# A two-layer diffusion step on one core: the first shift row summed on VectorE, the later conditioning rows turned to columns one tile later

## The chip, the cores and the metric

The kernel runs on one core of a Trainium2 chip. The metric is the device time of one execution in microseconds; the time given for a kernel is the median of several runs. One further execution is recorded by the hardware profiler, and every row quoted here is from such a recording. A core has five engines that work through lists of their own: TensorE (PE, with its weight loads as PEld), VectorE (DVE), ScalarE (ACT), GpSimd (POOL) and SyncE (SP, which here issues the loads). They wait for each other by semaphores only.

## The reference

One inference step of a model with two layers on 1024 latent and 128 context tokens of width 1024. Layer 0 mixes with a bidirectional gated linear recurrence, layer 1 with attention; each is followed by a squared-ReLU MLP. What matters here is how the conditioning enters: each layer makes six rows of 1024 from a condition vector, two of them (shift and scale) ahead of each norm and one (gate) behind each branch.

```python
def adaln_params(cond, w_ada, b_ada):
    mod = jax.nn.silu(cond) @ w_ada + b_ada
    return jnp.split(mod, 6, axis=-1)

def modulate(h, shift, scale):
    return h * (1 + scale[:, None, :]) + shift[:, None, :]

for l in range(DEPTH):
    sh1, sc1, g1, sh2, sc2, g2 = adaln_params(cond, ada_w[l], ada_b[l])
    h = modulate(rms_norm(x, norm_mix[l]), sh1, sc1)
    x = x + g1[:, None, :] * mixer(h)
    h = modulate(rms_norm(x, norm_mlp[l]), sh2, sc2)
    x = x + g2[:, None, :] * sq_relu_mlp(h, mlp_w1[l], mlp_w2[l])
```

There are two condition vectors, one for the latent and one for the context tokens. In the text "row j" is row j of layer 0: 0 shift and 1 scale ahead of the recurrence, 2 its gate, 3 and 4 shift and scale ahead of the MLP, 5 its gate.

## The kernel before, in words

Activations lie transposed: 128 partitions by 8 blocks of the width, and the 1152 tokens in three chunks of 384. A dense product runs three float32r matmuls for each 128x128 block (L120, L123, L124): weights and activations are split into a high and a low part (`whi`/`wlo`, `hhi`/`hlo`). Weights come as 512 KB pieces (`raw`, L88), are split on ScalarE (L93) and on VectorE or GpSimd (L95), and are prefetched in the order in which they are used.

The code is traced in program order; the framework's scheduler then writes each engine's list and hands out the buffers of each tag, and an instruction that needs a buffer waits until one is released. Two tags matter. `bank` (L126) hands out the eight PSUM banks. `unit` (L487) hands out twelve buffers of 128x1152 in the first layer's recurrent half; there nearly all that is not an activation chunk takes one: the squares and their sums, the conditioning weights, the gates' tensors and the copied rows.

**Two ways to make a conditioning row.** On TensorE: `ada_mm` (L162) multiplies both condition vectors, held as columns `cs`, with a tile of 128 inputs by 1024 outputs (`ada_n`); eight such tiles sum up in two banks with two rows of 512 each. `ada_rows` (L169) then copies each bank to SBUF (ScalarE, L175), turns it into columns with four transposes (TensorE, L178) and adds the bias (`mod_finish`, VectorE, L199 and L202). On VectorE: `ada_dot` (L142) takes a tile of 128 outputs by 1024 inputs (`ada_wt`) and multiplies it with the condition vector, broadcast over the partitions as `cb`, with a running sum; there is one such instruction for each of the two conditions, and the result is a column at once.

**Start** (`first_half`, L401). The first chunk of `x` is loaded, squared and summed; then for k from 0 to 7 the weights of row 1 and row 0 are loaded (L429) and multiplied on TensorE. Within that loop the chunk's `rstd` (L220, matmuls at L226) is worked out at k = 2 and spread over the partitions (L254) at k = 4. `ada_rows` for row 1 and for row 0 follows, then `modulate` (L266) writes `hhi` (ScalarE, L278) and `hlo`, and the first dense groups begin.

**Recurrent stage** (`rglru`, L490). There are eight tiles n of 128 state channels. In each, TensorE runs a dense group x (n + 1), two chunk groups y, and the gates of tile n (`gates`, L522). After the gates' matmuls stand ScalarE's exponentials (L545), tanh (L550) and roots (L559), and VectorE's products and scans (L567). At the end of the tile `ada_pe(3)` (L181) takes the next three of the 24 weight tiles of rows 2, 3 and 4, through two buffers `adaw` (L184). So row 2 is complete in tile 2 (its eighth weight tile is the second of the three), row 3 in tile 5 (first of the three) and row 4 in tile 7. When a row is complete, `ada_rows` runs at once. The last groups y 6 and 7 of each chunk and the split of the products into `zhi` and `zlo` close the stage.

All other rows, row 5 of layer 0 and the six of layer 1, are made on VectorE during the output projection and the MLP (`ada`, L149), with `cb` loaded and passed through Silu in `rg_out` (L647, L648).

Of the kernel before, what the change touches and what calls it, by code (L numbers as in the profile page):

```python
# [7 lines left out]
F32 = mybir.dt.float32  # L8
F32R = mybir.dt.float32r
I32 = mybir.dt.int32  # L10
AF = mybir.ActivationFunctionType
# [4 lines left out]
D = 1024  # L16
# [36 lines left out]
ADA_PE = [(_j, _k) for _j in (2, 3, 4) for _k in range(8)]  # L53


class Emit:
# [85 lines left out]
    def ada_dot(self, w, l, j, k, *conds):  # L142
        for cond in conds:
            self.nc.vector.scalar_tensor_tensor(  # L144
                out=w if cond else self.junk, in0=w, scalar=1.0, in1=self.cb[:, cond],
                op0=ALU.mult, op1=ALU.mult, accum_out=self.mod[:, l, j, cond, k:k + 1],
            )

# [17 lines left out]
                ps[i][0:2], lhsT=self.cs[:, :, k], rhs=w[:, i * 512:(i + 1) * 512], start=(k == 0), stop=(k == 7)  # L166
            )

    def ada_rows(self, l, j, ps):  # L169

        nc = self.nc
        psm = self.bank(16)
        for i in range(2):
            srow = self.unit("srow")[0:2, :512]
            nc.scalar.copy(out=srow, in_=ps[i][0:2])  # L175
            for k in range(4):
                o = 2 * (4 * i + k)
                nc.tensor.transpose(psm[:, o:o + 2], srow[:, k * 128:(k + 1) * 128], self.ident[0:2, 0:2])  # L178
        self.mod_finish(l, j, psm)

    def ada_pe(self, n):  # L181
        for j, k in self.pe_jobs[:n]:
            w = self.rgt.tile([128, 1024], F32, tag="adaw", name="adaw", bufs=2)
            self.nc.sync.dma_start(w, self.I["ada_n"][j, k * 128:(k + 1) * 128])  # L184
            if k == 0:
                self.ada_ps = [self.bank(512) for _ in range(2)]
            self.ada_mm(self.ada_ps, w, k)
            if k == 7:
                self.ada_rows(0, j, self.ada_ps)
        del self.pe_jobs[:n]  # L190

    def mod_finish(self, l, j, ps=None):
# [208 lines left out]
    def first_half(self, stop):  # L401
        nc, tc, I = self.nc, self.tc, self.I
        self.rgt = self.alloc(name="rgt", bufs=1, side="right")
        self.cells = None
        self.pe_jobs = list(ADA_PE)
        self.cs = self.rgt.tile([128, 2, 8], F32, name="cs")
        nc.scalar.activation(out=self.cs, in_=self.v("cond", 0, 16), func=AF.Silu)
        xs, sts = [], [{} for _ in range(NCH)]
        H = []

        def load_x0(c):
            x = self.cbig(F32, "x0")
            nc.sync.dma_start(x, I["xt"][c])
            xs.append(x)

        def square(c, ks=range(KT)):
            for k in ks:
                self.sq_acc(sts[c], xs[c][:, k], k)

        def hpair():  # L420
            H.append((self.cbig(F32R, "hhi"), self.cbig(F32R, "hlo")))

        load_x0(0)
        square(0)
        ps = [[self.bank(512) for _ in range(2)] for _ in range(2)]
        for k in range(8):
            for j in (1, 0):
                w = self.unit("ada")[:, :1024]
                nc.sync.dma_start(w, I["ada_n"][j, k * 128:(k + 1) * 128])  # L429
                self.ada_mm(ps[j], w, k)  # L430
            if k == 2:
                y = self.rstd(sts[0], D)
            if k == 4:
                r = self.spread(y)
        self.prefetch(2)
        load_x0(1)
        load_x0(2)
        self.ada_rows(0, 1, ps[1])
        self.ada_rows(0, 0, ps[0])
        hpair()  # L440
        for k in range(KT):
            self.modulate(0, xs[0], r, 0, 0, *H[0], ks=[k])
            if k >= 4:
                square(1, [k - 4])
        self.prefetch(3)
        square(1, range(4, 8))
        square(2)
        hpair()
        hpair()
        gens = [None] + [self.norm_mod(c, xs[c], sts[c], 0, 0, *H[c]) for c in (1, 2)]  # L450
        for g in gens[1:]:
            next(g)
        self.rglru(H, gens)
        self.rg_out(H, stop)
# [35 lines left out]
    def rglru(self, H, gens):  # L490
        nc = self.nc
# [83 lines left out]
        def finish(n, c, eng):  # L575
            eng.tensor_tensor(
                out=hs[c][:, n], in0=hs[c][:, n], in1=states[n][:, c * CH:(c + 1) * CH], op=ALU.mult
            )
# [13 lines left out]
        for c in range(NCH):  # L592
            ps = [self.bank() for _ in range(2)]
# [8 lines left out]
            ps = self.bank()  # L602
# [24 lines left out]
        self.Z = []  # L627
        for c in range(NCH):
            self.group([(n, pos["y", n], range(8)) for n in (6, 7)], rhs, yb_drain, chunks=[c])
            for m in (6, 7):  # L630
                finish(m, c, nc.vector)
            hi, lo = self.cbig(F32R, "zhi"), self.cbig(F32R, "zlo")
            for n in range(8):
                self.split(hi[:, n], lo[:, n], hs[c][:, n])
            self.Z.append((hi, lo))

    def rg_out(self, H, stop):
        nc, I, O = self.nc, self.I, self.O
        hs = self.hs
        nc.sync.dma_start(O["fin"], self.fin)  # L640
        self.release(*reversed(self.opened[1:]))
        self.wpx = self.alloc(name="wpx", bufs=1, side="right", reuse_waits="tile")
        self.cells = self.alloc(name="cells1", bufs=3, side="right", reuse_waits="tile")
        cbp = self.alloc(name="cb2", bufs=1, side="right", reuse_waits="tile")
        self.xp = self.alloc(name="xp", bufs=3, side="right", reuse_waits="tile")
        self.cb = cbp.tile([128, 2, 1024], F32, name="cb")
        nc.sync.dma_start(self.cb, I["crow"].to_broadcast([128, 2, 1024]))  # L647
        nc.scalar.activation(out=self.cb, in_=self.cb, func=AF.Silu)  # L648
        self.junk = cbp.tile([128, 1024], mybir.dt.bfloat16, name="junk")
        pi = len(RG_STREAM)  # L650
        self.prefetch(pi + 4)
        self.X = []
        for c in range(NCH):
            self.load_x(I["xt"], c)
        H2 = self.out_proj(pi, self.Z, 0, 2)
        pi += 8
        if stop == 1:
            self.need(None)
            for c in range(NCH):
                nc.sync.dma_start(O["yt"][c], self.X[c])  # L660
            return
        sts = [{} for _ in range(NCH)]
        self.H3 = []

        def after(c):
            hi, lo = self.cbig(F32R, "hhi"), self.cbig(F32R, "hlo")
            nc.sync.dma_start(self.xmid[c], self.X[c])
            self.H3.append((hi, lo))
            yield from self.norm_mod(c, self.X[c], sts[c], 1, 0, hi, lo)

        self.pi = self.mlp(pi, 0, H2, lambda c, m: self.sq_acc(sts[c], self.X[c][:, m], m), after)
        self.cbp = cbp
        if stop == 2:
            self.need(None)
            for c in range(NCH):
                nc.sync.dma_start(O["yt"][c], self.X[c])
# [530 lines left out]
```

## Time and profile before

| | us |
|---|---|
| median of 3 runs | 2876.45 (2875.54 to 2877.26) |
| the profiled execution | 2874.78 |
| its span, first to last instruction | 2873.0 |
| TensorE busy in the span | 2766.8 |
| VectorE, ScalarE, GpSimd busy | 1386.7, 1156.0, 478.1 |
| mean granted TensorE clock | 0.984 |

In a row of the timeline stand the start, the length (both in us), the engine, the line, the operation, output<-input, the shape and the number of instructions merged in the row; in brackets the engine's idle time before it and what ended it. In a row of the waits stand who waited for whom, the total in us, the times, and the longest. SPq rows are SyncE's issues of loads; in a row of the issues stand the number, the size and the median time from issue to landing. The GB/s row has the queue's rate in 40 equal slices of the first 50 us.

### The profile page before, as it was taken

What the parts mean: (1) busy time and instruction counts of PE and PEld (TensorE: products, weight loads), DVE (VectorE), ACT (ScalarE), POOL (GpSimd) and SP (SyncE); (2) the same over time, 40 slices, a digit from 0 to 9 for tenths busy, and PEclk for the clock granted to TensorE, in tenths of its full rate; (3) what the DMA queues carried; (4) which work ended last, traced back from release to release, by engine and by line L of the source; (5) the groups of instructions that cost most, each with busy time, mean ns of one, the idle gap of its engine ahead of it and who ended that gap; (6) DMA issues with size and microseconds to landing.
All of it is one profiled execution on the core that took longest, in us unless ns stands there. A gap on an engine that the chain in (4) does not pass through costs nothing. (4 is left out here: it accounts for less than half of the span.)

```text
span 2873.0 us, 39932 instructions
## 1 busy us (share of the span) xinstructions
PE 2766.8 (96%) x16163; PEld 2684.7 (93%) x16163; DVE 1386.7 (48%) x2774; ACT 1156.0 (40%) x2193; POOL 478.1 (17%) x247
## 2 busy tenths in 40 slices
PE   7989898999999999998997999999999999999998
PEld 3878698999999999998997999999999999999998
DVE  4787676645435442327354766661732222223225
ACT  3667742422331232234335877771423312322332
POOL 1000013112111121212241000001221121212121
PEclk9999999999999999999998999999999999999999
DMA  5122242222223131112155212125011110101111
GB/s 237 45 81 81 69 151 96 70 78 85 92 70 100 66 103 38 54 57 89 59 157 181 76 57 82 48 82 187 30 52 38 39 50 30 59 30 52 37 45 67
DMA packets 79177, 223.88 MB, mean 78 GB/s; under 512 B 7824, under 2 KB 36304, under 8 KB 77328
## 3 DMA queue, kind: packets, MB, share of 16 engines
q1 hardware_dynamic: 78224, 218.18, 22.3%
q0 software_dynamic: 768, 3.15, 0.3%
q8 instruction: 127, 2.08, 0.3%
q14 instruction: 58, 0.48, 0.1%
HBM read 185.47 MB, written 33.20 MB: 76 GB/s over the span
## 5 line engine op out<-in xcount | busy, mean ns | idle before, releaser
L95 POOL TENSOR_TENSOR wlo<-raw,whi 128x1024 fp32r<-128x1024 f32 x161 | 390.4, 2425 | 2041.0 <-ACT whi L93 2041.0
L120 PE MATMUL ps<-hhi,whi 128*128 128x384 f32 x2088 | 701.8, 338 | 1.9 <-ACT hhi L278 1.9
L123 PE MATMUL ps<-hlo,whi 128*128 128x384 f32 x2088 | 702.7, 337 | 0.1
L124 PE MATMUL ps<-hhi,wlo 128*128 128x384 f32 x2088 | 702.0, 336 | 0.0
L93 ACT CAST whi<-raw 128x1024 fp32r<-128x1024 f32 x181 | 190.2, 1052 | 869.9 <-PE ps L123 736.3
L120 PE MATMUL ps<-hid,whi 128*128 128x384 f32 x1536 | 516.2, 336 | 0.0
L123 PE MATMUL ps<-hid,whi 128*128 128x384 f32 x1536 | 515.5, 336 | 0.0
L124 PE MATMUL ps<-hid,wlo 128*128 128x384 f32 x1536 | 515.4, 336 | 0.0
L288 DVE SCALAR_TENSOR_TENSOR X<-ps,mod,X 128x256 f32<-128x256 f32 (+1 forms) x576 | 281.0, 513 | 481.7 <-PE ps L124 445.1
L120 PEld LDWEIGHTS ps<-hhi,whi 128*128 128x128 f32 x2088 | 393.7, 189 | 10.3 <-issue 4.3
L123 PEld LDWEIGHTS ps<-hlo,whi 128*128 128x128 f32 x2088 | 394.1, 189 | 4.0 <-issue 3.5
L124 PEld LDWEIGHTS ps<-hhi,wlo 128*128 128x128 f32 x2088 | 394.0, 189 | 0.3 <-DVE wlo L95 0.3
L139 DVE TENSOR_TENSOR hid<-cell,hid 128x384 fp32r<-128x384 f32 x192 | 141.8, 742 | 491.3 <-ACT hid L138 491.2
L120 PEld LDWEIGHTS ps<-hid,whi 128*128 128x128 f32 x1536 | 288.9, 188 | 0.0
L123 PEld LDWEIGHTS ps<-hid,whi 128*128 128x128 f32 x1536 | 288.8, 188 | 0.0
L124 PEld LDWEIGHTS ps<-hid,wlo 128*128 128x128 f32 x1536 | 288.7, 188 | 0.0
L343 ACT ACTIVATE cell<-ps 128x384 f32<-128x384 f32 x192 | 93.6, 489 | 304.6 <-PE ps L124 304.6
L144 DVE SCALAR_TENSOR_TENSOR junk<-raw,cb 128x1024 bf16<-128x1024 f32 x56 | 96.1, 1716 | 118.9 <-DMA raw<-ada_wt 118.9
L930 ACT ACTIVATE p<-ps,nm 128x384 f32<-128x384 f32 (+1 forms) x200 | 112.9, 576 | 37.9 <-DVE nm L925 37.8
L139 DVE TENSOR_TENSOR pt<-ps,pt 128x384 fp32r<-128x384 f32 (+1 forms) x200 | 106.6, 543 | 37.2 <-ACT pt L138 36.8
L915 DVE TENSOR_REDUCE mx<-ps 128x1 f32<-128x384 f32 (+1 forms) x200 | 107.8, 539 | 27.7 <-PE ps L914 27.0
L344 ACT ACTIVATE cell<-cell 128x384 f32<-128x384 f32 x192 | 100.6, 525 | 5.9
(182 smaller groups left out, 4094.5 us busy)
## 6 DMA issues: line engine op xcount, KB each, us to landing
raw<-wts SPq DMA_DIRECT2D x181, 512.0 KB, 3.3
raw<-ada_wt SPq DMA_DIRECT2D x56, 512.0 KB, 3.3
adaw<-ada_n SPq DMA_DIRECT2D x24, 512.0 KB, 4.0
qn_d<-qn SPq DMA_DIRECT2D x12, 768.0 KB, 5.5
q<-qn_d SPq DMA_DIRECT2D x16, 576.0 KB, 5.0
ada<-ada_n SPq DMA_DIRECT2D x16, 512.0 KB, 10.2
o_d<-o SPq DMA_DIRECT2D x64, 128.0 KB, 1.7
x<-xt SPq DMA_DIRECT2D x3, 1536.0 KB, 10.4
```

What stands on the lines that cost most here:

```text
L93: nc.scalar.copy(out=hi, in_=raw)
L95: eng.tensor_tensor(out=lo, in0=raw, in1=hi.bitcast(F32), op=ALU.subtract)
L120: mm = nc.tensor.matmul(ps, lhsT=w[0], rhs=h[0], start=first, stop=False)
L123: nc.tensor.matmul(ps, lhsT=w[0], rhs=h[1], start=False, stop=False)
L124: nc.tensor.matmul(ps, lhsT=w[1], rhs=h[0], start=False, stop=last)
L139: (lo_eng or nc.vector).tensor_tensor(out=lo, in0=src, in1=hi.bitcast(F32), op=ALU.subtract)
L144: self.nc.vector.scalar_tensor_tensor(out=w if cond else self.junk, in0=w, scalar=1.0, in1=self.cb[:, cond], op0=ALU.mult, op1=ALU.mult, a ...
L288: self.nc.vector.scalar_tensor_tensor(out=self.X[c][:, m, a:b], in0=ps[:, a:b], scalar=self.mod[:, l, j, cond, m:m + 1], in1=self.X[c][:, ...
L343: nc.scalar.activation(out=r, in_=ps, func=AF.Relu)
L344: nc.scalar.activation(out=r, in_=r, func=AF.Square)
L915: nc.vector.tensor_reduce(out=mx[:, j:j + 1], in_=ps, axis=AX.X, op=ALU.max)
L930: nc.scalar.activation(out=p[:, j * CH:j * CH + w], in_=ps, func=AF.Exp, scale=SCALE, bias=nm[:, 1:2], accum_out=sm[:, j:j + 1],)
```

## The change

Row 0 (shift) is no longer summed on TensorE but with `ada_dot` on VectorE, from `ada_wt`, in the same loop over k in which TensorE sums row 1. For this the two broadcast condition vectors `cb` are loaded at the start, one tile each, and passed through Silu on ScalarE; they and `junk`, where one of the two dots writes its products, take three of the twelve `unit` buffers. The chunk's `rstd` moves ahead of the loop. `ada_rows` is cut in two: the copy to SBUF (now one tile of 1024 for both halves) and `ada_cols`, the eight transposes and the bias. For row 1 both follow each other as before. For rows 2, 3 and 4 the copied row is kept in `self.rows`, and the transposes run at the beginning of the next `ada_pe`, one tile later; for row 4 after the first group of the closing y loop. In `rg_out`, `cb` becomes a list of two views of the same tile.

```diff
     def ada_dot(self, w, l, j, k, *conds):
         for cond in conds:
             self.nc.vector.scalar_tensor_tensor(
-                out=w if cond else self.junk, in0=w, scalar=1.0, in1=self.cb[:, cond],
+                out=w if cond else self.junk, in0=w, scalar=1.0, in1=self.cb[cond],
                 op0=ALU.mult, op1=ALU.mult, accum_out=self.mod[:, l, j, cond, k:k + 1],
             )
...
-    def ada_rows(self, l, j, ps):
-
-        nc = self.nc
+    def ada_rows(self, ps):
+        srow = self.unit("srow")[0:2, :1024]
+        for i in range(2):
+            self.nc.scalar.copy(out=srow[:, i * 512:(i + 1) * 512], in_=ps[i][0:2])
+        return srow
+
+    def ada_cols(self, l, j, srow):
+
         psm = self.bank(16)
-        for i in range(2):
-            srow = self.unit("srow")[0:2, :512]
-            nc.scalar.copy(out=srow, in_=ps[i][0:2])
-            for k in range(4):
-                o = 2 * (4 * i + k)
-                nc.tensor.transpose(psm[:, o:o + 2], srow[:, k * 128:(k + 1) * 128], self.ident[0:2, 0:2])
+        for k in range(8):
+            self.nc.tensor.transpose(
+                psm[:, 2 * k:2 * k + 2], srow[:, k * 128:(k + 1) * 128], self.ident[0:2, 0:2]
+            )
         self.mod_finish(l, j, psm)
 
+    def ada_late(self):
+        for j, srow in self.rows:
+            self.ada_cols(0, j, srow)
+        self.rows = []
+
     def ada_pe(self, n):
+        self.ada_late()
         for j, k in self.pe_jobs[:n]:
...
             if k == 7:
-                self.ada_rows(0, j, self.ada_ps)
+                self.rows.append((j, self.ada_rows(self.ada_ps)))
         del self.pe_jobs[:n]
...
         load_x0(0)
+        self.cb = [self.unit("cb")[:, :1024] for _ in range(2)]
+        for i in range(2):
+            nc.sync.dma_start(self.cb[i], I["crow"][:, i].to_broadcast([128, 1024]))
+            nc.scalar.activation(out=self.cb[i], in_=self.cb[i], func=AF.Silu)
+        self.junk = self.unit("junk")[:, :1024]
         square(0)
-        ps = [[self.bank(512) for _ in range(2)] for _ in range(2)]
+        y = self.rstd(sts[0], D)
+        ps = [self.bank(512) for _ in range(2)]
         for k in range(8):
-            for j in (1, 0):
-                w = self.unit("ada")[:, :1024]
-                nc.sync.dma_start(w, I["ada_n"][j, k * 128:(k + 1) * 128])
-                self.ada_mm(ps[j], w, k)
-            if k == 2:
-                y = self.rstd(sts[0], D)
+            w = self.unit("ada")[:, :1024]
+            nc.sync.dma_start(w, I["ada_n"][1, k * 128:(k + 1) * 128])
+            self.ada_mm(ps, w, k)
+            w = self.unit("adat")[:, :1024]
+            nc.sync.dma_start(w, I["ada_wt"][0, k * 128:(k + 1) * 128])
+            self.ada_dot(w, 0, 0, k, 0, 1)
             if k == 4:
                 r = self.spread(y)
         self.prefetch(2)
         load_x0(1)
         load_x0(2)
-        self.ada_rows(0, 1, ps[1])
-        self.ada_rows(0, 0, ps[0])
+        self.ada_cols(0, 1, self.ada_rows(ps))
+        self.mod_finish(0, 0)
...
             self.group([(n, pos["y", n], range(8)) for n in (6, 7)], rhs, yb_drain, chunks=[c])
+            self.ada_late()
```

More of the change, by code (lines that the diff above doesn't have):

```diff
@@ L404, in first_half @@
         self.cells = None
-        self.pe_jobs = list(ADA_PE)
+        self.pe_jobs, self.rows = list(ADA_PE), []
         self.cs = self.rgt.tile([128, 2, 8], F32, name="cs")
@@ L645, in rg_out @@
         self.xp = self.alloc(name="xp", bufs=3, side="right", reuse_waits="tile")
-        self.cb = cbp.tile([128, 2, 1024], F32, name="cb")
-        nc.sync.dma_start(self.cb, I["crow"].to_broadcast([128, 2, 1024]))
-        nc.scalar.activation(out=self.cb, in_=self.cb, func=AF.Silu)
+        cb = cbp.tile([128, 2, 1024], F32, name="cb")
+        nc.sync.dma_start(cb, I["crow"].to_broadcast([128, 2, 1024]))
+        nc.scalar.activation(out=cb, in_=cb, func=AF.Silu)
+        self.cb = [cb[:, i] for i in range(2)]
         self.junk = cbp.tile([128, 1024], mybir.dt.bfloat16, name="junk")
```

## The prediction, before the change was run

> **What bounds the kernel now.** I read the page's busy table first, then the windows (25 us stretches), then TensorE's waits, then the timeline around the steps that the change touches.
>
> ```profile
> PE 2766.8 (96%) x16163; PEld 2684.7 (93%) x16163; DVE 1386.7 (48%) x2774; ACT 1156.0 (40%) x2193; POOL 478.1 (17%) x247
> 25.00:50.00 25.00, 23.55 (x79) 6.51 (x76) 4.01 (x21) 3.56 (x6) 0.00 (x0) 1.00 0.73 295
> 175.00:200.00 25.00, 16.55 (x63) 9.85 (x63) 20.86 (x23) 15.46 (x19) 0.00 (x0) 0.80 0.20 64
> 225.00:250.00 25.00, 25.00 (x133) 21.99 (x132) 22.94 (x24) 16.77 (x21) 0.00 (x0) 1.00 0.26 85
> 275.00:300.00 25.00, 15.31 (x82) 13.44 (x80) 18.56 (x22) 20.19 (x27) 0.00 (x0) 0.91 0.19 64
> PE ps L178 <- ACT srow L175: 20.2, 3, 11.1
> PE ps L165 <- DMA adaw<-ada_n: 4.9, 2, 3.0
> ```
>
> TensorE is busy for 2766.8 of 2873.0 us, so only some 106 us are idle, and only idle TensorE time or removed TensorE work can be won. Columns of a window row are busy us of PE, PEld, DVE, ACT and POOL, then the granted clock, the DMA share and GB/s. A step of the recurrent stage (225 to 250) keeps TensorE full; 175 to 200 and 275 to 300 do not, and the granted clock falls there too. The waits between 60 and 900 us name the cause: the transposes of L178 wait 20.2 us in three places for `srow`, ScalarE's copy of a conditioning row.
>
> **Part 1: the first two rows.** The timeline of TensorE and VectorE, and of the loads:
>
> ```profile
> 16.13 11.93 PE L165 MATMUL ps<-ada,cs 128*2 128x512 f32 x24 [16.13 <-DMA ada<-ada_n]
> 28.00 1.50 PE L226 MATMUL ps<-ones,acc 128*128 128x2 f32 x12
> 36.86 10.46 PE L165 MATMUL ps<-ada,cs 128*2 128x512 f32 x24
> 47.94 0.24 DVE L199 TENSOR_TENSOR mod<-ps,vec 128x8 f32<-128x8 f32 x2 [16.07 <-PE ps L178]
> 49.40 0.23 DVE L199 TENSOR_TENSOR mod<-ps,vec 128x8 f32<-128x8 f32 x2
> 49.59 1.63 ACT L278 ACTIVATE hhi<-cell,mod 128x384 fp32r<-128x384 f32 x3 [1.05 <-DVE mod L199]
> GB/s 0 125 192 364 393 377 400 446 462 452 383 393 419 416 406 403 410 410 416 410 403 410 410 416 406 406 426 446 442 403 380 406 410 403 118 0 0 0 0 20
> ada<-ada_n SPq DMA_DIRECT2D x16, 512.0 KB, 10.2
> raw<-ada_wt SPq DMA_DIRECT2D x56, 512.0 KB, 3.3
> adaw<-ada_n SPq DMA_DIRECT2D x24, 512.0 KB, 4.0
> 573.45 1.23 DVE L144 SCALAR_TENSOR_TENSOR junk<-raw,cb 128x1024 bf16<-128x1024 f32 x1 [3.60 <-DMA raw<-ada_wt]
> 574.72 1.22 DVE L144 SCALAR_TENSOR_TENSOR raw<-raw,cb 128x1024 f32<-128x1024 f32 x1
> 448.13 2.03 DVE L144 SCALAR_TENSOR_TENSOR junk<-raw,cb 128x1024 bf16<-128x1024 f32 x1 [2.96 <-DMA raw<-ada_wt]
> L648 ACT ACTIVATE cb<-cb x1: 1917/1917/1917, 402.9 to 402.9; 128x2048 f32<-128x2048 f32 x1
> 44.78 0.57 ACT L175 COPY srow<-ps 2x512 f32<-2x512 f32 x1 [30.97 <-PE ps L165]
> ```
>
> Before: sixteen 512 KB tiles pass through TensorE, four matmul instructions each. From 36.86, 24 of them take 10.46 us, 0.43 each, so a tile costs 1.72 us and the stage 27.5 us. The queue fills these 16.13 to 47 us at about 410 GB/s, a tile (0.52 MB) in 1.28 us: TensorE, not the queue, is the bound. The shift row is finished at 49.40 and releases the first `hhi`.
>
> Removed: eight tiles of TensorE, 13.7 us. Added on VectorE: sixteen dots. Two on one tile run from 573.45 to 575.87, 2.5 us with nothing beside them, so 8 x 2.5 = 20 us; they lie in VectorE's 16.07 us hole and the time before. Added on the queue: the two `cb` loads, 1.05 MB or 2.56 us, issued ahead of the weights on SP; the row-wise tiles cost it what the old ones did. Added on ScalarE: two Silu, 1.92 us together by L648's row, hidden in its 30.97 us hole before 44.78; without that cover the dots would begin that much later. Moved: the first chunk's `rstd` (28.00, 1.5 us of TensorE in the middle of the stage) comes ahead of the weights, into the time in which TensorE waits for the first one.
>
> So the first tile lands at 16.13 + 2.56 = 18.7 and the first row-wise tile at 20.0. A pair takes 2 x 1.28 = 2.56 on the queue, 2.5 on VectorE and 1.72 on TensorE, so the queue paces all three. The last row-wise tile lands at 20.0 + 7 x 2.56 = 37.9, its dots end at 40.4. TensorE's last tile lands at 36.6, is through at 38.4, and its copies (two of 0.57), transposes and the scale's finish take some 2 us: 40.5, the same moment. The first `hhi` comes at about 41.4 instead of 49.59: **8.2 us won**. Bounds: nothing, if dots or matmuls run at the worst rates below; 12 us, if the `x` and `raw` loads that now precede the weights on SP come after them (1.5 MB of `x` and one 0.5 MB piece are 4.9 us). Behind the weights on SP stand `x` chunk 2, two pieces and the first `adaw` loads; they go out about when they do now, since the last weight's issue stays some 10.2 us ahead of its landing (37.9), as its row has it.
>
> A rule that speaks against this: the Trainium skill, "TensorE: Matmul & The Clock Gate", Part 1, says that the clock is granted in windows of about 3.4 us and falls to half after an idle one. Here TensorE would pause 0.84 us in each 2.56, and the window 25 to 50 holds 1.00 with pauses of that size; by the rule too the clock stays. A second page, "DMA: Bandwidth & Descriptors", Bandwidth, sets HBM to SBUF at about 358 GB/s for a core; by that figure a pair takes 2.93 us and the win would be some 5.5 us as an estimate, but the queue's row shows 400 and more, and I keep it.
>
> **Part 2: the later rows.** Row 2 ends in recurrent tile 2, row 3 in tile 5, row 4 in tile 7.
>
> ```profile
> 178.05 3.60 PE L165 MATMUL ps<-adaw,cs 128*2 128x512 f32 x8
> 179.96 15.19 SPq L184 DMA_DIRECT2D adaw<-ada_n  x3
> 181.19 1.34 ACT L545 ACTIVATE A<-tr,sp 128x1152 f32<-128x1152 f32 x1
> 187.36 2.22 ACT L559 ACTIVATE tr<-tr 128x1152 f32<-128x1152 f32 x2
> 189.48 1.04 ACT L175 COPY srow<-ps 2x512 f32<-2x512 f32 x2
> 190.61 1.87 PE L165 MATMUL ps<-adaw,cs 128*2 128x512 f32 x2
> 196.73 0.34 PE L120 MATMUL ps<-hhi,whi 128*128 128x384 f32 x1
> 288.44 1.88 PE L165 MATMUL ps<-adaw,cs 128*2 128x512 f32 x4
> 300.82 1.04 ACT L175 COPY srow<-ps 2x512 f32<-2x512 f32 x2
> 304.25 3.51 PE L165 MATMUL ps<-adaw,cs 128*2 128x512 f32 x6
> 307.70 0.44 PE L120 MATMUL ps<-hhi,whi 128*128 128x384 f32 x1
> 361.90 1.88 PE L165 MATMUL ps<-adaw,cs 128*2 128x512 f32 x4 [3.04 <-DMA adaw<-ada_n]
> 364.46 0.41 PE L178 MATMUL ps<-ident,srow 2*128 2x2 f32 x4 [0.68 <-ACT srow L175]
> 364.79 0.44 PE L120 MATMUL ps<-hhi,whi 128*128 128x384 f32 x1
> 228.31 1.88 PE L165 MATMUL ps<-adaw,cs 128*2 128x512 f32 x4
> 267.65 0.67 ACT L500 ACTIVATE xf<-ps,vec 128x384 f32<-128x384 f32 x1
> 305.36 2.34 DVE L567 TENSOR_TENSOR_SCAN tr<-A,vec,ti 128x1024 f32<-128x1024 f32 x1
> 10.35 3.41 POOL L218 TENSOR_TENSOR acc<-acc,cell 128x384 f32<-128x384 f32 x3 [9.90 <-ACT cell L216]
> ```
>
> In tile 2 TensorE has its row at 178.05 + 8 x 0.43 = 181.5. ScalarE's list holds the gates' exponentials (181.19) and roots (187.36) ahead of the copies, which come at 189.48. From the restart, two matmul instructions take 1.8 us from 190.61 instead of 0.86; only at 196.73 is the old pace back. Between 181.5 and 196.73, 15.2 us, lie eight transposes (0.33 us for four, 364.46 to 364.79), four ada instructions and six others of 0.174: 0.66 + 1.72 + 1.04 = 3.4 us. **11.8 us** are lost. Tile 5: from 288.44 + 1.72 = 290.2 to 307.70, 17.5 us, of which eight transposes and eight ada instructions are 4.1: **13.4 us**. Tile 7: 363.6 to 364.79 with 0.33 of work: **0.9 us**. Together 26.1.
>
> Moved, the transposes stand ahead of the next tile's ada matmuls, after its gates: by then some 30 us have passed, and `srow` is long there. Their cost (0.66 per row) stays. What is late next is a load: tile 2's third ada tile is issued when the first one's buffer comes free, 179.96, and lands 4.0 us later (the median of the `adaw` issue row above) at 184.0, while TensorE arrives at 181.5. Where ten matmuls of other work stand in between (tile 3, 228.31, no wait) it is covered; tile 2's third job starts a new row with new PSUM banks, so I count 2.4 us against the win (all of TensorE's list waits behind it), and nothing for tile 5. DVE and ACT run 23 and 17 us in a full 25 us window, so neither becomes the bound. **26.1 - 2.4 = 23.7 us won**; bounds 12 (one stall returns) and 27.
>
> **The sum.** The profiled execution took 2874.78 us, 1.78 more than its span. 2874.78 - 8.2 - 23.7 = 2842.9. The median of the runs shown is 1.7 higher; I take **2844**. About 0.2%, some 6 us, is what a measurement of this kernel can tell from no change.
>
> **Rivals.**
>
> *Only the stalls go (2852).* Beside a busy GpSimd a dot took 2.03 us (448.13) instead of 1.23; at that price a pair is 3.3 us on VectorE, eight end at 46.5, and 2 us are won. Or TensorE stays cold, 0.9 us an instruction as at 190.61: 32 of them from 18.7 end at 47.5. Against it: GpSimd's adds end at 13.8 (10.35 + 3.41).
>
> *A stall comes back as a buffer wait (2856 to 2868).* `srow` now holds one of the twelve `u` buffers for a tile step, and its two PSUM banks stay taken until ScalarE's copies, beside the next row's two, which leaves four of eight. In tile 5 the next `xf` then gets a buffer only when the first scans (305.36) have freed theirs, where in a quiet tile `xf` is written well ahead of them (267.65). ScalarE stands at that copy until about 308; TensorE, at a group of 24 matmuls and one bank in 4.2 us, needs all four to cover 292 to 308. With fewer it waits again, up to the 12 us of one stall or both.
>
> *The change does not do what it says (2866).* The transposes could still stand where TensorE waits, if ScalarE's list puts the copies later still; only part 1 is won. Little speaks for it: a whole tile lies between.
>
> *Slower: the twelve buffers starve the first loads (2899).* Two `cb`, `junk` and the eight tiles of the squares are eleven of twelve. If their buffers do not come back, the sixteen loads pass through one: 3.3 us to land (the `ada_wt` issue row) plus about 2.1 in use, 5.4 x 16 = 86 us from about 11, so 97 instead of 49.4: 48 lost, 24 won elsewhere. At two buffers the stage ends at 54 and the whole is still faster; below two it decides. Against it: GpSimd's adds, which free three of them, are over by 13.8, and VectorE's free three more.
>
> **How the numbers follow.** Forecast 0.66 (2834 to 2852), only the stalls 0.14, buffer wait 0.11, not what it says 0.04, slower 0.05. Faster by over 0.2% takes the first three, less a share in which two of them meet, and most of the fourth: 0.87; within 0.07; slower 0.06. The range reaches from the twelve of part 1 with all of part 2 (2835, less 2) to a buffer wait: 2833 to 2862.
>
> **What would show it.** Right: no L178 row waiting for `srow`; window clocks of 1.00 around the old 190 and 301; the first `hhi` near 41 us; dots of 1.23 us ending near 40; a wait of some 2 us for `adaw` in tile 2. Wrong: dots of 2 us, matmuls of 0.9 us between 20 and 40, `xf` copies released by a scan with TensorE idle beside them, or new waits after 400 us, where I expect the old ones, only earlier.

## The result, and the profile after

| | before | after |
|---|---|---|
| median, us (lowest to highest, 4 runs each) | 2876.06 (2875.54 to 2877.26) | 2843.47 (2842.33 to 2843.63) |
| ratio, 95% interval | | 0.9882 [0.9868, 0.9896] |
| profiled execution, span | 2874.78, 2873.0 | 2843.63, 2841.9 |

The kernel is 32.6 us faster; 2844 was forecast. The number was right, its parts less so. The busy table of the kernel after (engine, busy us, share, instructions), its windows, and TensorE's waits between 60 and 900 us:

```profile
PE 2749.7 (97%) x16123; PEld 2679.4 (94%) x16123; DVE 1403.4 (49%) x2806; ACT 1158.3 (41%) x2194; POOL 483.1 (17%) x247
```

```profile
25.00:50.00 25.00, 17.81 (x43) 4.84 (x44) 22.56 (x44) 4.32 (x8) 0.00 (x0) 0.87 0.87 348
175.00:200.00 25.00, 22.71 (x113) 18.21 (x112) 20.98 (x21) 17.35 (x22) 0.00 (x0) 1.00 0.19 64
...
275.00:300.00 25.00, 25.00 (x125) 20.02 (x124) 19.81 (x19) 20.13 (x25) 0.00 (x0) 1.00 0.27 85
350.00:375.00 25.00, 21.14 (x113) 20.82 (x112) 18.03 (x39) 12.22 (x25) 11.39 (x3) 0.93 0.16 60
```

```profile
PE ps L165 <- DMA adaw<-ada_n: 4.1, 3, 1.9
PE ps L124 <- POOL wlo L95: 3.9, 1, 3.9
```

The wait for `srow` (20.2 us in three places) is gone, and the windows 175 to 200 and 275 to 300 hold a clock of 1.00. New is a wait of 3.9 us for GpSimd's `wlo`; it lies in the window 350 to 375, the beginning of the output projection, and lowers the clock there.

Where the time went, from the first instruction of each stage in the two traces: the first `hhi` came at 49.59 and comes at 46.80 (2.8 us won); the first matmul of the output projection at 390.4 and 361.7 (28.7); the first matmul of the MLP at 563.8 and 536.7 (27.1); layer 1's first query projection (`cq`) at 1428.3 and 1401.2 (27.1); attention's first store (`o_d`) at 1570.3 and 1537.6 (32.7); the spans end 31.1 apart. So the start won 2.8, the recurrent stage 25.9; the output projection gave back 1.6; the way into attention won 5.6; from there to the end 1.6 were lost.

**The start, after.** The loads as SyncE issued them, then ScalarE, VectorE and TensorE in the timeline:

```profile
5.01 0.46 SPq L443 DMA_DIRECT2D ada<-ada_n  x1
5.52 0.55 SPq L446 DMA_DIRECT2D adat<-ada_wt  x1
8.76 0.33 SPq L422 DMA_DIRECT2D x<-xt  x1
11.67 0.33 SPq L443 DMA_DIRECT2D ada<-ada_n  x1
```

```profile
10.54 1.28 ACT L436 ACT_TABLE_LOAD   x1
11.84 2.00 ACT L436 ACTIVATE cb<-cb 128x1024 f32<-128x1024 f32 x2
13.74 1.75 ACT L225 ACTIVATE cell<-x 128x384 f32<-128x384 f32 x4
...
19.46 0.16 DVE L242 TENSOR_SCALAR sv<-ps 128x3 f32<-128x3 f32 x1 [3.24 <-PE ps L235]
...
23.73 1.22 DVE L144 SCALAR_TENSOR_TENSOR junk<-adat,cb 128x1024 f32<-128x1024 f32 x1
...
41.53 1.88 PE L165 MATMUL ps<-ada,cs 128*2 128x512 f32 x4 [0.68 <-DMA ada<-ada_n]
...
44.62 1.23 DVE L144 SCALAR_TENSOR_TENSOR adat<-adat,cb 128x1024 f32<-128x1024 f32 x1
...
46.80 1.67 ACT L287 ACTIVATE hhi<-cell,mod 128x384 fp32r<-128x384 f32 x3 [1.69 <-DVE cell L283]
```

Two things are late. On SyncE, the third chunk of `x` (8.76) has slipped ahead of 14 of the 16 weights: the second pair had no buffer until the squares gave theirs back. Its 1.57 MB are 3.8 us at 410 GB/s, and TensorE's last tile starts at 41.53. On VectorE, the chain to `rstd` (from 19.46, with two weight splits between its steps) comes to its last step at 23.65, and the sixteen dots run from 23.73 to 45.85. That chain begins late because ScalarE does the table load and the two Silu for `cb` (10.54 to 13.84) in the middle of the chunk's squares, the last four of which begin at 13.74.

**The recurrent stage and the output projection, after.** First TensorE; then GpSimd and TensorE at the output projection, and the group of GpSimd's splits (number, then shortest, median and longest in ns):

```profile
174.56 3.60 PE L165 MATMUL ps<-adaw,cs 128*2 128x512 f32 x8
180.05 1.88 PE L165 MATMUL ps<-adaw,cs 128*2 128x512 f32 x4 [1.89 <-DMA adaw<-ada_n]
181.85 0.44 PE L120 MATMUL ps<-hhi,whi 128*128 128x384 f32 x1
...
281.44 1.88 PE L165 MATMUL ps<-adaw,cs 128*2 128x512 f32 x4
283.25 0.44 PE L123 MATMUL ps<-hlo,whi 128*128 128x384 f32 x1
...
308.78 0.65 PE L179 MATMUL ps<-ident,srow 2*128 2x2 f32 x8
309.36 3.17 PE L165 MATMUL ps<-adaw,cs 128*2 128x512 f32 x7
...
335.80 1.88 PE L165 MATMUL ps<-adaw,cs 128*2 128x512 f32 x4 [0.57 <-DMA adaw<-ada_n]
```

```profile
361.49 8.73 POOL L95 TENSOR_TENSOR wlo<-raw,whi 128x1024 fp32r<-128x1024 f32 x1 [23.30 <-DVE zlo L139]
...
370.28 0.44 PE L124 MATMUL ps<-zhi,wlo 128*128 128x384 f32 x1 [3.86 <-POOL wlo L95]
```

```profile
L95 POOL TENSOR_TENSOR wlo<-raw,whi x161: 2339/2395/8734, 331.5 to 2773.4; 128x1024 fp32r<-128x1024 f32 x161
```

Tile 2 goes from its last ada matmul straight on, after 1.89 us for the third tile's load; tile 5 without a pause. Row 3's transposes (308.78) stand ahead of tile 6's ada matmuls and wait for nothing. The second weight piece of the output projection (GpSimd splits the first at 331.5) takes 8.73 us, against a median of 2.40, while VectorE writes `zlo`; it is over at 370.22, and TensorE goes on at 370.28.

### The profile page after: what moved, and what is told of

Its sections match the earlier page's. It is cut to its first block, busy times and chain, and to the rows that moved or that the text cites. A ratio compares the mean times of both kernels' runs of the same rounds, so it can differ in the third digit from the quotient of the medians.

```text
span 2841.9 us, 39879 instructions
## 1 busy us (share of the span) xinstructions
PE 2749.7 (97%) x16123; PEld 2679.4 (94%) x16123; DVE 1403.4 (49%) x2806; ACT 1158.3 (41%) x2194; POOL 483.1 (17%) x247
## 5 line engine op out<-in xcount | busy, mean ns | idle before, releaser
L95 POOL TENSOR_TENSOR wlo<-raw,whi 128x1024 fp32r<-128x1024 f32 x161 | 396.1, 2461 | 2009.0 <-ACT whi L93 1976.9
## 6 DMA issues: line engine op xcount, KB each, us to landing
x<-xt SPq DMA_DIRECT2D x3, 1536.0 KB, 14.1
X<-xt SPq DMA_DIRECT2D x3, 1536.0 KB, 11.8
```

The lines of the kernel that those rows point to most:

```text
L95: eng.tensor_tensor(out=lo, in0=raw, in1=hi.bitcast(F32), op=ALU.subtract)
```

## The experiments

Each is compared with runs of the kernel before on the same chip; the gain at a stage is read from one profiled execution against the first profile of the kernel before.

**Each part alone.** e1 is the kernel before with the rows' transposes late; the start is the old one. e2 is the kernel after with the transposes at once:

```diff
-                self.rows.append((j, self.ada_rows(self.ada_ps)))
+                self.ada_cols(0, j, self.ada_rows(self.ada_ps))
```

> Part 2 alone: rows 2, 3 and 4 are turned to columns one tile later, the start is that of the kernel before. First theory (the stalls are worth what the prediction counted, and the start has little to do with the gain): the three waits of the transposes for srow are gone, layer 0 ends some 24 us earlier, and the time is 2852 us, or 2848 if the 4 us that the changed kernel wins later, at the start of attention, come with it. Rival (a good part of the 32 us comes from the start): not under 2860 us.

> Part 1 alone: row 0 on VectorE, rows 2, 3 and 4 turned to columns at once. First theory (the start won 2.8 us, first hhi at 46.8 instead of 49.6, and no more): 2873 us, 2869 if the 4 us at the start of attention come with it; the waits for srow are there again with 8 and 11 us. Rival (the start won the 8.2 us of the prediction, and lost them again behind it): 2868 us with a first hhi at 41.

e1: 2851.52 us (2849.32 to 2853.60), ratio 0.9914 [0.9900, 0.9927]; 24.8 us by the medians, 24.6 at the first matmul of the output projection. The rows alone give what the first theory expected.

e2: 2862.19 (2861.40 to 2869.27), ratio 0.9955 [0.9943, 0.9968]; both theories missed. The first `hhi` came at 46.6 (3.0 won), not at 41, and 2.2 us were left at the output projection, as expected; but 14 us were won in all. The rest came later: the output projection took 167.0 us where the kernel before took 173.4, and the way into attention 135.7 where it took 142.0. From the recurrent stage's end on, the two kernels' lists are the same on all engines. SyncE's own waits between 340 and 410 us, in the kernel before and in e2, show one difference:

```profile
SPq L647 <- DVE hs L576: 6.0, 1, 6.0
```

```profile
SPq L663 <- DVE hs L591: 0.5, 1, 0.5
```

The load of `cb` for the later rows waits 6.0 us for a buffer that `hs` holds, and all loads behind it wait with it; in e2 it gets one that is free 5.5 us sooner, and TensorE's later wait for `wlo` (1.9 us before) is not in e2's list. That the start's three more buffers moved the turn of the twelve is my reading; it was not tried, and e1, whose start has none of them, has neither of these two waits. The two gains so add up to more than the kernel after has (24.8 + 14.1 against 32.6), above all since it has the new wait where e2 wins its 6.4.

**The start: queue or VectorE.** e4 lays both `cb` and `junk` into one tile of the activation chunks' tag, so that they take none of the twelve buffers. e5 also holds the `x` chunks 1 and 2 behind the weights. e10 is e5 with half-length dots for row 0 (half of that row's sum is left out).

```diff
-        self.cb = [self.unit("cb")[:, :1024] for _ in range(2)]
+        cbj = self.cbig(F32, "cbj").rearrange("p a b -> p (a b)")
+        self.cb = [cbj[:, i * 1024:(i + 1) * 1024] for i in range(2)]
...
-        self.junk = self.unit("junk")[:, :1024]
+        self.junk = cbj[:, 2048:3072]
...
+        load_x0(1, True)
+        load_x0(2, True)
         self.prefetch(2)
-        load_x0(1)
-        load_x0(2)
```

```diff
+        n = 512 if (l, j) == (0, 0) else 1024
...
-                out=w if cond else self.junk, in0=w, scalar=1.0, in1=self.cb[cond],
+                out=(w if cond else self.junk)[:, 0:n], in0=w[:, 0:n], scalar=1.0, in1=self.cb[cond][:, 0:n],
```

> The whole change, but cb and junk lie in one activation chunk's buffer, so that the ring of twelve has three more for the weights. The list of loads then has x chunk 2 behind the sixteen weights again, 1.57 MB or 3.8 us of the queue. If the queue alone sets the end of the start, the first hhi comes 3.8 us earlier than in the changed kernel (43.0) and the time is 2839.7 us. If VectorE sets it, which begins its dots only at 23.7 us behind the first chunk's rstd and needs 2.55 us for a pair, they end at 44.1, the first hhi comes at 45.1 and the time is 2841.8. If the ring has nothing to do with it: 46.8 and 2843.5.

> As the run with cb elsewhere, and both later x chunks are pinned behind the sixteen weights in the list of loads. There VectorE set the end of the start: its sixteen dots ran without a gap from 23.4 to 43.4 us, because rstd and two splits stand ahead of them. With one x chunk less ahead, the first pair lands some 3 us earlier. If VectorE's list is what counts and the dots may begin before rstd, they begin near 19 and the first hhi comes at 41 to 42 (2839 us); if rstd stays ahead of them, nothing moves: 44.4 and 2841.7.

> This is the kernel after with both changes to the loads of the start (the cb rows in a tile of their own, x chunks 1 and 2 behind the weights), and in it the 16 dots of layer 0's first shift row run over the first 512 of their 1024 inputs; the other half of that row's sum is left out. Theory (VectorE, whose dots run without a pause of its own in that kernel, sets the start): the dots end about 10 us earlier, TensorE's scale row, done at 37.8 us there, becomes the last, and the first hhi comes at 38.5 to 40 us in place of 43.9; the time falls by 4 to 5 us, to about 2838. Rival (the queue of loads or ScalarE's chain to rstd sets the start, and the dots only end with it): the first hhi stays at 43 to 44 us and the time at 2842.5.

e4: 2841.74 (2839.09 to 2842.74), ratio 0.9877 [0.9862, 0.9892]; first `hhi` at 44.4. The third chunk of `x` is back behind the weights, so it was the buffers that let it slip: in the kernel after SyncE's issues of weights wait 2.5 us for the sum of the squares on VectorE and 1.1 for that on GpSimd, and in e4 for neither. e5: 2842.53 (2838.76 to 2844.15), 0.9882 [0.9867, 0.9896]; first `hhi` at 43.9. TensorE's timeline and VectorE's in e5, then the same in e10:

```profile
33.72 2.98 PE L165 MATMUL ps<-ada,cs 128*2 128x512 f32 x6
...
41.76 1.22 DVE L144 SCALAR_TENSOR_TENSOR adat<-adat,cbj 128x1024 f32<-128x1024 f32 x1
...
44.60 1.01 PE L120 MATMUL ps<-hhi,whi 128*128 128x384 f32 x2 [6.83 <-ACT hhi L287]
```

```profile
33.48 4.03 PE L166 MATMUL ps<-ada,cs 128*2 128x512 f32 x9
...
37.05 0.69 DVE L145 SCALAR_TENSOR_TENSOR adat<-adat,cbj 128x512 f32<-128x512 f32 x1
...
39.77 2.19 ACT L288 ACTIVATE hhi<-cell,mod 128x384 fp32r<-128x384 f32 x4 [1.65 <-DVE cell L284]
```

With the queue clear in e5, TensorE has its row at 36.7, its columns at 37.8, and then waits 6.83 us for VectorE's last dots. With dots of 0.69 us (e10) the first `hhi` comes at 39.8, 4.2 earlier, and TensorE's row is the last; 2837.43 (2834.53 to 2841.47), 0.9869 [0.9853, 0.9886]. That VectorE's dots set the start in e5 is so shown. The runs of e4 and e5 overlap those of the kernel after (2842.33 to 2846.34 with the repeat below), so what they win is read from the first `hhi` alone.

**One stall back.** e6 turns row 3 alone at once, in tile 5:

```diff
                 self.rows.append((j, self.ada_rows(self.ada_ps)))
+                if j == 3:
+                    self.ada_late()
```

> The whole change, but row 3 is turned to columns at once, as before. One stall is put back alone: the transposes of tile 5 wait some 11 us for srow, and TensorE runs at half pace for some us behind it. If the stall costs what the prediction took for it (wait and slow pace, 13.4 us), the time is 2857 us; if only the wait counts, 2854.6; if other waits would have taken its place anyway, under 2849.

2855.85 (2854.66 to 2858.52), ratio 0.9930 [0.9918, 0.9943]: 12.4 us more than the kernel after (11.0 more than its repeat). Its waits between 60 and 340, TensorE in tile 5, and the window:

```profile
PE ps L179 <- ACT srow L172: 11.1, 1, 11.1
```

```profile
289.46 0.58 PE L179 MATMUL ps<-ident,srow 2*128 2x2 f32 x4 [11.12 <-ACT srow L172]
289.98 1.87 PE L165 MATMUL ps<-adaw,cs 128*2 128x512 f32 x2
```

```profile
275.00:300.00 25.00, 13.88 (x53) 7.30 (x53) 19.76 (x20) 14.83 (x17) 0.00 (x0) 0.80 0.25 85
```

The wait is 11.1 us, and two ada instructions behind it take 1.87, twice the 0.43 us each of the quiet stage. By the first matmul of the output projection 14.4 us are lost (12.6 against the repeat), so the wait does not account for all of it.

**Do the kept rows starve others?** e7 lets each kept row hold two of the twelve buffers (two tiles of 512 in place of one of 1024).

> The whole change, but each kept row holds two of the twelve buffers for a tile instead of one. It doubles the suspected cost of the rival in which a stall comes back as a wait for a buffer. If holding a buffer costs nothing, 2843.5 us and the tiles 3 to 7 as in the changed kernel; if one held buffer already costs TensorE time, two cost more: over 2847, with ScalarE's xf copies of tiles 5 and 6 released by scans and TensorE idle beside them.

2844.37 (2842.53 to 2845.52), ratio 0.9889 [0.9874, 0.9904]; the runs overlap those of the kernel after, and no new wait appears. Holding a second buffer costs nothing here. The two PSUM banks were not varied.

**The new wait.** e8 lets VectorE split the first three pieces of the output projection; e9 adds e5's two edits.

```diff
-            eng = nc.vector if self.piece_i < len(RG_STREAM) else nc.gpsimd
+            eng = nc.vector if self.piece_i < len(RG_STREAM) + 3 else nc.gpsimd
```

> The whole change, and the first three weight pieces of the output projection are split on VectorE instead of GpSimd. In the changed kernel TensorE waits 3.9 us there for GpSimd's split and then runs at half pace for some 4 us; before the change it did not. If that wait is a price of the earlier arrival, it goes, with the half pace: 5 to 6 us, 2838 us. Rival (VectorE has its own work there, and TensorE waits for zlo instead): 2843 us.

> The whole change with cb elsewhere, both later x chunks behind the weights, and the three splits on VectorE. If the effects add: the time of the x-behind run less that of the moved splits, 2833 to 2836 us. If the splits gain nothing: the time of the x-behind run.

e8: 2837.68 (2836.31 to 2839.63), ratio 0.9869 [0.9852, 0.9885]. The second and third of the three splits on VectorE, and the window:

```profile
362.44 1.22 DVE L95 TENSOR_TENSOR wlo<-raw,whi 128x1024 fp32r<-128x1024 f32 x1
...
364.51 1.22 DVE L95 TENSOR_TENSOR wlo<-raw,whi 128x1024 fp32r<-128x1024 f32 x1
```

```profile
350.00:375.00 25.00, 25.00 (x147) 25.00 (x146) 20.78 (x44) 16.45 (x29) 3.47 (x1) 1.00 0.42 173
```

TensorE is full from 350 to 375 and the gain at the MLP's first matmul is 34.4 in place of 27.1. e9: 2837.82 (2834.01 to 2839.07), 0.9865 [0.9850, 0.9880]; its profiled start and output projection add up (37.0 at the MLP), its median does not differ from e8's. Both are faster than the kernel after: their slowest runs lie below its fastest.

Why did the same split not stop TensorE in the kernel before? There GpSimd and VectorE met the other way round:

```profile
386.14 6.03 DVE L139 TENSOR_TENSOR zlo<-hs,zhi 128x384 fp32r<-128x384 f32 x8
...
389.00 2.75 POOL L95 TENSOR_TENSOR wlo<-raw,whi 128x1024 fp32r<-128x1024 f32 x1 [24.65 <-ACT whi L93]
...
455.88 0.58 PE L124 MATMUL ps<-zhi,wlo 128*128 128x384 f32 x1 [1.86 <-POOL wlo L95]
```

The split took 2.75 us, and VectorE's eight passes 6.03 in place of 3.83. In the kernel after VectorE kept its pace (six passes in 2.90 us from 365.13, over at 368.03) and the split ended 2.19 us behind them. The last row is another wait for a split, later in the stage, which the kernel after no longer has.

**The spread, and attention's entry.** The kernels after and before once more.

> The kernel after once more, for the spread of one kernel beside the others of this call. Both theories: 2842 to 2844 us, first hhi at 46.8 us, the wait for GpSimd's piece in the output projection again near 3.9 us, and attention's entry (cq to o_d) at 136.4 us within 1 us. If the entry comes nearer to the kernel before's 142 us, then the gain seen there belongs to the run and not to the kernel.

> The kernel before once more, for its profile. If the 5 to 6 us that attention's entry (first load of cq to first store of o_d) takes less in the kernel after belong to the kernels, the entry takes 142 us within 1 us again, against 136.4 and 136.5 us in two profiles of the kernel after. Rival (it belongs to the one profiled execution): 137 to 139 us here, and an execution of about 2869 us. Either way the recurrent stage's two waits for a conditioning row and the output projection (first matmul of zhi to first of hid, 173.4 us) come again within 1 us.

After: 2844.83 (2844.44 to 2846.34), ratio 0.9894 [0.9879, 0.9909]; all four runs lie over the 2842 to 2844 that were expected, with the first `hhi` (46.5) and the `wlo` wait (3.8) nearly as in the first profile. Before: 2878.38, one run. From the first `cq` matmul to the first store of `o_d` the kernel before takes 142.0 and 142.1 us, the kernel after 136.4 and 136.5. So the 5.6 us come again with each kernel. The output projection of the kernel before took 175.1 us in this profile, against 173.4, where less than 1 us was expected: that stage moves by 1.7 from run to run, and its loss of 1.6 above says nothing by itself. VectorE and GpSimd at the point where the entry first differs, in the kernel before and then after:

```profile
1424.88 2.61 DVE L139 TENSOR_TENSOR ckv<-cell,ckv 128x384 fp32r<-128x384 f32 x2
...
1425.93 1.16 POOL L713 TENSOR_TENSOR raw_p<-raw_p,cos 128x384 f32<-128x384 f32 x1
...
1431.08 2.42 POOL L95 TENSOR_TENSOR wlo<-raw,whi 128x1024 fp32r<-128x1024 f32 x1 [2.71 <-ACT whi L93]
...
1431.17 2.75 DVE L715 TENSOR_TENSOR raw_p<-raw_p,cell 128x384 f32<-128x384 f32 x1
```

```profile
1397.77 1.80 DVE L139 TENSOR_TENSOR ckv<-cell,ckv 128x384 fp32r<-128x384 f32 x2
...
1400.71 1.02 POOL L730 TENSOR_TENSOR raw_p<-raw_p,cos 128x384 f32<-128x384 f32 x1 [2.02 <-DMA cell<-raw_p]
...
1405.38 0.55 DVE L732 TENSOR_TENSOR raw_p<-raw_p,cell 128x384 f32<-128x384 f32 x1
```

The instructions and their order are the same. In the kernel before GpSimd's products begin behind its split almost at once and run beside VectorE's pass, which takes 2.61 us; in the kernel after they wait 2.02 us for a copy, and the pass takes 1.80. Later one product of VectorE takes 2.75 us beside a split, and 0.55 in the kernel after, where however a step of 128x3 is held for 1.90 (1403.56).

These meetings are not the whole of it. Followed along TensorE's list, the lead of the kernel after is 27.1 us at the entry, 28.0 by 1444, 30.1 by 1538, and the last 2.6 us come at one place. There TensorE waits for ScalarE's `p` in both kernels and then goes on at different paces, in the kernel before and then after:

```profile
1552.69 0.90 PE L966 MATMUL ps<-ident,p 128*128 128x128 f32 x3 [2.97 <-ACT p L951]
...
1553.71 0.52 PE L911 MATMUL ps<-k,q 128*128 128x384 f32 x1
```

```profile
1522.63 0.55 PE L983 MATMUL ps<-ident,p 128*128 128x128 f32 x3 [2.97 <-ACT p L968]
...
1523.37 0.34 PE L929 MATMUL ps<-k,q 128*128 128x384 f32 x1
```

The granted clock is 0.50 from 1553 to 1558 in the kernel before, and 1.00 from 1523 to 1528 in the kernel after. All thirteen profiles have this wait (2.96 or 2.97 us). Half pace follows it in the two profiles of the kernel before and in e6 (entries of 142.0, 142.1 and 138.3 us), a little later in e1 (139.1), and not in the nine others (135.7 to 136.6). So nearly half of the 5.6 us is TensorE's clock. That the meetings of GpSimd and VectorE make up the other 3.0 is argued, not shown by a run; why the copy lands later, and why the same wait has two effects, is open.

## Why the prediction came out

**Part 2 was right.** Forecast 23.7, measured 25.9 in the stage (23.8 in the second profile of the kernel after) and 24.8 alone (e1). Tile 2: 9.0 won by the two timelines, forecast 11.8 less 2.4; the wait for the third load was 1.89. Tile 5: 13.1, forecast 13.4. Tile 7: 3.1, forecast 0.9, since its wait for `adaw` fell from 3.04 to 0.57. The buffer wait did not come: e7 holds twice as many buffers and loses nothing. That the late transposes do it is shown by e6, where one of them put back costs 12.4.

**Part 1 was wrong: 2.8 us, not 8.2.** Two steps of it failed. The first is "Behind the weights on SP stand `x` chunk 2": it went ahead of 14 of them. I had its price, 3.8 us for a chunk, among the bounds, and had counted the eleven of twelve buffers, but drew from that only that the loads might starve, not that a later load with a buffer of another tag would go first. e4, with the buffers back, has the chunk behind the weights and wins 2.4 of it. The second is "A pair takes 2 x 1.28 = 2.56 on the queue, 2.5 on VectorE and 1.72 on TensorE, so the queue paces all three". The paces were right (the last four tiles of TensorE start 2.56 apart, the dots take 1.22), but with 2.5 against 2.56 VectorE can never make up a late start, and its dots begin at 23.7, behind `rstd` and two splits, not at 20.0. Both hold the first `hhi` back: with the queue clear it comes at 43.9 (e5), and with the dots cut as well at 39.8 (e10), where 41.4 was forecast.

Two terms behind these steps were also off. The two Silu were put at nothing, "hidden in its 30.97 us hole"; with their table load they took 3.3 us of ScalarE among the squares, ahead of `rstd`. And the first weight tile landed at 20.0, not 18.7: the loads ahead of it, the two of `cb` among them, ran at 272 GB/s between 7.5 and 8.75 us, where the kernel before has 400. No run moved these two alone. Two slips in the sums change no conclusion: 2842.9 and 1.7 are 2844.6, and the rivals' 2866 and 2899 leave that 1.7 out.

**The clock.** Expected to stay at 1.00 in the start. It was 0.66 between 25 and 30 us, behind a wait of 1.79 for a load, and 1.00 from 30 to 45 with pauses of 0.64 to 0.68. The window of the kernel before from which the forecast was read has no pause of 0.84 us in its weight stage: TensorE is busy there without a break until 48.1. The first tile's matmuls took 0.81 us each and those of the next three 0.58, but from 33.85 on TensorE waits for each tile's load again, so it cost nothing.

**What was not seen.** "New waits after 400 us, where I expect the old ones, only earlier" stands under wrong in the prediction, and the output projection, which now begins at 361.7, has a new one (at 366) and has lost an old one. Along TensorE's list the lead of the kernel after falls from 28.7 to 23.0 us at the new wait (3.86 us and the slow matmuls behind it), and rises to 27.0 where the kernel before waits 1.86 us and then runs slow (455.88); the forecast lacks both. e8, without the new wait, gains 6.2 us in that stage, about what e2 gains there (6.4). The forecast also lacks the 5.6 of attention's entry. Against the forecast the sum of the gains is off by -5.4 in the start, +2.2 in the recurrent stage, -1.6 in the output projection, +5.6 at the entry and -1.6 behind it, together -0.8. So the total came out partly by luck: errors of 5 us in both directions cancelled, and the 5.6 hang in part on TensorE's clock at one wait. The parts are what to learn from. The rival "Only the stalls go" came nearest for the start (2 us), but not by its reason: no dot was slowed, all took 1.22 us.

## What to carry to other kernels

Two paces that nearly agree (2.50 and 2.56 us a pair) hide no start: work out when each engine can begin, not only how fast it goes. When a change takes buffers of a ring, look for the loads that do not use that ring; they go out first and take the queue. And a copy that stands behind long work on its own engine is best read one step later, ahead of work that does not need it: e6 puts 12.4 us on one such place.

## What the runs showed of the hardware

GpSimd's split of a 128x1024 piece has a median of 2.40 us and took 8.73 beside VectorE's passes of `zlo`; those did not change (six in 2.90 us from 365.13 beside the split, eight in 3.83 in e8 with GpSimd idle: 0.48 each). In the kernel before it was VectorE that was held at this place, and at the attention entry too, 2.75 us in place of 0.55. The Trainium skill, "GPSIMD Engine Reference", Key points, says that the two share their SBUF interfaces and contend where a VectorE instruction has two inputs in SBUF. `zlo` is such an instruction, and the trace agrees; which of the two is held here, and for how long, is read from the rows.

Stalls of TensorE of 8.5 and 11.1 us (in the kernel before; 11.1 in e6 too) were followed by matmuls at half pace, 0.9 us in place of 0.43. For shorter waits the length alone did not decide. One of 1.89 us in tile 2 was followed by full pace (its window has 1.00), one of 1.86 at 455.88 in the kernel before by matmuls of 0.52 us in place of 0.34, and the wait of 2.97 at attention's entry by either.
